# Sums of weights for seven-product tiles, made in DRAM by added transfers

## The chip, the cores and the metric

The kernel runs on one core of one Trainium2 chip. The metric is device microseconds from the start to the end of one execution; the time shown is the median of several runs. A profile is one further execution, taken by the hardware profiler, and its span runs from the first to the last instruction of the core.

Engines are named as in the profile: PE is TensorE, DVE VectorE, ACT ScalarE, POOL GpSimd, SP SyncE. SP and POOL are used here only as queues that issue DMA transfers.

## The reference, cut to what matters

A decoder layer on x of 512 tokens by 1024 channels, all in float32:

```python
f = swiglu(rms_norm(h, ffn1_norm_pre), ffn1_w_gate, ffn1_w_up, ffn1_w_down)
h = h + 0.5 * rms_norm(f, ffn1_norm_post)

u = rms_norm(h, mix_norm_pre)
proj = u @ w_in                     # q, k, v of 12 heads, xr, yr, two gates
...                                 # dilated attention in 3 groups, merged; RG-LRU recurrence
h = h + rms_norm(merged @ w_out, mix_norm_post)

f = swiglu(rms_norm(h, ffn2_norm_pre), ffn2_w_gate, ffn2_w_up, ffn2_w_down)
h = h + 0.5 * rms_norm(f, ffn2_norm_post)

def swiglu(x, w_gate, w_up, w_down):
    return (jax.nn.silu(x @ w_gate) * (x @ w_up)) @ w_down
```

The inner width of each feed-forward is 2816, that is 22 tiles of 128 columns (f = 0 to 21), each with 128 columns of `w_gate` and 128 of `w_up`.

## The kernel before, in words

**Precision by splitting.** Each float32 operand is split into a rounded part and a rest (`split`: ACT copies to a 32-bit format with fewer bits, DVE subtracts), and a product is made of three matmuls: high by high, high by low, low by high. So all weights pass ACT and DVE before PE reads them.

**Seven products in place of eight.** Most tiles with two weight blocks (gate and up of a feed-forward tile; pairs of columns of `w_in`) are computed in Strassen-Winograd fashion. The two blocks and the two halves of the depth give four quarters of weights, u0, u1, g0, g1, each 128 x 512 as stored; two halves of the tokens and the two halves of the depth give four quarters of activations. `seven` makes seven products (p1, p2, p6, p5, p7, p4, p3 in this order, 12 matmuls of 256 columns each) in place of eight. It needs forms of the weights: u0+u1, u0+u1+g0, u0+u1+g0+g1, u0+g0, and g0, g1 (in the kernel before, p4 takes u1 and p3 the sum of all four). `w_forms(key)` makes them: one load of all four quarters (1 MB) into a buffer `raw`, four VectorE adds of 128 x 512 (lines 567, 568, 569 and 572), some of them in place in `raw`, and splits into three buffers `w8` and one `w4`. There are 51 such tiles: 17 in the first feed-forward (f = 5 to 21), 16 pairs in the mixers, 18 in the second feed-forward (f = 4 to 21). `NSTD` gives the number of tiles of each feed-forward that are computed plainly.

**Stages, in order.** First feed-forward (`ffn(1, ...)`), ended by `last_product`: the last down-projection, whose result is multiplied by a row of gains on DVE, added to the residual h, normalised and transposed (`Boundary`: `block`, `turn`). Then attention (`values`, `qk`, `attend` for four heads, `seven` tiles for the gates), the recurrence (`conv`, `branch`, `gates_of`, `recur`), the output projection with the second `Boundary`, and the second feed-forward. In a feed-forward the order is that of `ffn_order`: the forms of tile f+1 are prepared ahead of the products of tile f; after some tiles one half of an earlier part's down-projection is done (`down`).

**Loads of weights.** All weights lie in one DRAM tensor `wst` (`in_w` in the profile) in the order of use; `raw_of` loads them group by group on SP's queue into a ring `raw` of two slots of 128 x 2048. A slot comes free when the last split or add that reads it is done. `w8` has four buffers, `w4` two.

**POOL's queue.** It issues only DMA transfers: at the end of the first feed-forward the residual (`h` from `in_xn`, line 745), two rows of gains (`gains`, line 397), the new residual to DRAM (`kept_m`, line 432), a reordering of the values of one group (line 812); after attention the residual back (line 981), and the same kinds of transfers around the second boundary.

**What sets the order.** The kernel is written for a planner. Instructions get numbers in the order in which the code issues them; a block under `tc.high_priority(offset=n)` gets numbers that are n lower. The planner plays the program through with costs of its own and gives each engine or queue, whenever it is free, the ready instruction with the lowest number. Ready means that what it reads has been written and that a buffer for what it writes is free. From this it fixes one order for each queue and the semaphore waits; on the chip each queue then runs strictly in that order. A DRAM tile of its own name and tag has its own place, and needs no other to be released.

Of the kernel before, what the change touches and what calls it, by code (L numbers as in the profile page):

```python
# [10 lines left out]
F32 = mybir.dt.float32  # L11
F32R = mybir.dt.float32r
AF = mybir.ActivationFunctionType
ALU = mybir.AluOpType
AX = mybir.AxisListType

P = 128
# [3 lines left out]
NF = 22  # L21
FF_PARTS = ((0, 4), (4, 8), (8, 12), (12, 16), (16, 22))
NSTD = {1: 5, 2: 4}
# [4 lines left out]
RAW_W = 2048  # L28
NEG = -1.0e30
AHEAD = 100  # L30
# [100 lines left out]
def stream_groups():  # L131

    groups, cur, w = [], [], 0
    for key, width in stream_plan():
        if w + width > RAW_W or (cur and cur[0][0][0] == "start"):
            groups.append(cur)
            cur, w = [], 0
        cur.append((key, w, width))
        w += width
    groups.append(cur)  # L140
    return groups
# [12 lines left out]
def hybrid_layer(ctx: ExitStack, tc: tile.TileContext, xT: bass.AP, xN: bass.AP, wst: bass.AP,  # L154
                 first: bass.AP, rows: bass.AP, consts: bass.AP, bias: bass.AP, out: bass.AP):
    nc = tc.nc
# [4 lines left out]
    wpool = ctx.enter_context(tc.tile_pool(name="wpool", bufs=4))  # L161
# [3 lines left out]
    dpool = ctx.enter_context(tc.tile_pool(name="dpool", bufs=1, space=bass.MemoryType.DRAM))  # L165
# [35 lines left out]
    groups = stream_groups()  # L201
    state = {"g": 0, "i": 0, "off": 0, "raw": None}

    def raw_of(key):

        g, i = state["g"], state["i"]
        grp = groups[g]
        if i == 0:
            w = grp[-1][1] + grp[-1][2]
            raw = wpool.tile([P, RAW_W], F32, name="raw", tag="raw", bufs=2)  # L210
            src = bass.AP(tensor=wst.tensor, offset=wst.offset + state["off"], ap=[[w, P], [1, w]])
            nc.sync.dma_start(raw[:, :w], src)
            state["raw"] = raw
            state["off"] += w * P
        k, o, w = grp[i]
        assert k == key, (k, key)
        src = state["raw"][:, o:o + w]
        if i + 1 == len(grp):
            state["g"], state["i"] = g + 1, 0
        else:  # L220
            state["i"] = i + 1
        return src

    def fetch(key, slot=None, ahead=0):

        with tc.high_priority(offset=ahead if slot else AHEAD):
            src = raw_of(key)
            w = src.shape[-1]
            t = slot() if slot else w8() if w > 512 else w4()
            split(t[:, 0, :w], t[:, 1, :w], src)  # L230
            return t[:, 0, :w], t[:, 1, :w]

    def w8():
        return wpool.tile([P, 2, 1024], F32R, name="w8", tag="w8", bufs=4)

    def w4():
        return wpool.tile([P, 2, 512], F32R, name="w4", tag="w4", bufs=2)
# [27 lines left out]
    def split(dh, dl, src):  # L265
        ACT.activation(dh, src, AF.Copy)  # L266
        DVE.tensor_sub(dl, src, dh.bitcast(F32))  # L267

    def acc_ps():
        return psum.tile([P, T], F32, name="acc", tag="acc", bufs=5)  # L270

    def aux_ps():
        return psum.tile([P, T], F32, name="aux", tag="aux", bufs=3)

    def tmp(name):
        return tpool.tile([P, T], F32, name=name, tag="t")
# [280 lines left out]
        return t, [early, middle, late]  # L557

    spool = [None]

    def w_forms(key):

        with tc.high_priority(offset=AHEAD):
            raw = raw_of(key)
            u0, u1, g0, g1 = (raw[:, i * 512:(i + 1) * 512] for i in range(4))
            s12 = spool[0].tile([P, 2, 512], F32, name="s12", tag="s", bufs=2)
            DVE.tensor_add(s12[:, 1, :], u0, u1)
            DVE.tensor_add(s12[:, 0, :], s12[:, 1, :], g0)
            DVE.tensor_add(u0, u0, g0)
            a, b, c, d = w8(), w8(), w8(), w4()  # L570
            split(a[:, 0, :], a[:, 1, :], raw[:, 1024:2048])
            DVE.tensor_add(g1, s12[:, 0, :], g1)  # L572
            split(b[:, 0, :], b[:, 1, :], s12.rearrange("p s c -> p (s c)"))
            split(c[:, 0, :], c[:, 1, :], raw[:, 0:1024])
            split(d[:, 0, :], d[:, 1, :], g1)
            lo, hi = slice(0, 512), slice(512, 1024)
            return {"p1": a[:, :, lo], "p2": a[:, :, hi], "p6": b[:, :, lo], "p5": b[:, :, hi],
                    "p7": c[:, :, lo], "p4": c[:, :, hi], "p3": d}
# [114 lines left out]
    def act_two(pool):  # L693

        ts = [pool.tile([P, 8, T], F32R, name="act", tag="act", bufs=3) for _ in range(2)]
        return Act([ts[0][:, k, :] for k in range(8)], [ts[1][:, k, :] for k in range(8)])
# [22 lines left out]
    u1 = act_two(ap1)  # L719
# [9 lines left out]
    for k in range(KC):  # L729
        wh, wl, raw = wts[k]  # L730
# [30 lines left out]
    with ExitStack() as mx:  # L761
# [14 lines left out]
        def values(g, first=False):  # L776
            if g:
                vals[g] = apool.tile([P, 4, T], F32, name="vals", tag=f"v{g}")
            else:
                vals[g] = tpl.tile([P, 8, T], F32, name="vals", tag="attn")[:, 0:4, :]  # L780
            ws = [fetch(("v", g, k)) for k in range(4)] if first else [None] * 4
            pss = [acc_ps() for _ in range(4)] if g != VALUES[1] else [aux_ps(), aux_ps(), aux_ps(), acc_ps()]

            def part(kk, bs):
                wh, wl = (w.rearrange("p (k c) -> p k c", k=2) for w in ws[kk])
                for b in bs:
                    bl = slice(b * P, (b + 1) * P)
                    for i in range(2):
                        k = 2 * kk + i
                        PE.matmul(pss[b], um.hi[k][:, bl], wh[:, i, :], start=k == 0, stop=False)  # L790
                        PE.matmul(pss[b], um.hi[k][:, bl], wl[:, i, :], start=False, stop=False)  # L791
                        PE.matmul(pss[b], um.lo[k][:, bl], wh[:, i, :], start=False, stop=k == KC - 1)  # L792

            if first:
                for b in range(4):
                    for kk in range(4):
                        part(kk, (b,))
                    if b < 2:
                        bd1.turn(b + 2)
                    ACT.activation(vals[g][:, b, :], pss[b], AF.Copy)  # L800
            else:
                for kk in range(4):
                    ws[kk] = fetch(("v", g, kk))
                    part(kk, range(4))
                for b in range(4):
                    ACT.activation(vals[g][:, b, :], pss[b], AF.Copy)
            if g == 0:

                nv = apool.tile([P, 4, T], F32, name="vals", tag="vn")
                for b in range(4):  # L810
                    for p in range(4):
                        nc.gpsimd.dma_start(nv[32 * p:32 * p + 32, b, :], vals[g][32 * b:32 * b + 32, p, :])
                vals[g] = nv

        t, steps = forms_of(um, um_t[:2], um_t[2:], apool, False)
        values(VALUES[0], True)
        attn_t = tpl.tile([P, 8, T], F32R, name="attn", tag="attn")
        attn = Act([attn_t[:, i, :] for i in range(4)], [attn_t[:, 4 + i, :] for i in range(4)])
        steps[0]()
        values(VALUES[1])  # L820
        steps[1]()
        values(VALUES[2])
        pairs = [[(g * 4 + hd, 12 + g * 4 + hd) for g in range(NG)] for hd in range(NH)]
# [140 lines left out]
            DVE.tensor_sub(attn.lo[hd], om, attn.hi[hd].bitcast(F32))  # L964

        for hd in range(NH):
            attend(hd, qkvs.pop(hd))
            if hd + 1 < NH:
                qkvs[hd + 1] = qk(hd + 1)


        for c in range(0, KC, 2):
            g, u = tmp("g"), tmp("u")
            seven(t, pair_of(("pair", 52 + c, 53 + c)), acc_ps()[:, :HB], [g[:, h] for h in HALVES],
                  [u[:, h] for h in HALVES])
            ACT.activation(facc[:, c, :], g, AF.Sigmoid)
            ACT.activation(facc[:, c + 1, :], u, AF.Sigmoid, scale=-1.0)
# [9 lines left out]
    with ExitStack() as mx:  # L987
# [10 lines left out]
        o, w = SMALL["ap"]  # L998
# [42 lines left out]
        def branch(hd):  # L1041

            gel = []
            for c in (2 * hd, 2 * hd + 1):
                ps = acc_ps()
                gemm(ps, fetch(("in", 44 + c)), um)
                ge = lpool.tile([P, T], F32, name="ge", tag="ge", bufs=4)
                with tc.high_priority(offset=EVAC):
                    DVE.tensor_copy(ge, ps)
                gel.append(ge)  # L1050
            return gel
# [47 lines left out]

        conv(0)  # L1100
        for hd in range(NH):
            gel = branch(hd)
            if hd + 1 < NH:
                conv(hd + 1)
            gas, gxs = gates_of(hd)
            recur(hd, gel, gas, gxs)
            for c in GATE1[hd]:
                ps = acc_ps()
                gemm(ps, fetch(("in", 60 + c)), um)
                ACT.activation(sig[:, c, :], ps, AF.Sigmoid)  # L1110
# [28 lines left out]
    grow5, _ = gains(ap2, 4)  # L1139
# [121 lines left out]
```

## Time and profile before

| | |
|---|---|
| median of 3 runs | 1248.76 us (1248.39 to 1249.63) |
| span of the profiled execution | 1246.4 us |
| PE busy | 1233.0 us (99%) |
| DVE busy | 913.5 us (73%) |
| ACT busy | 670.4 us (54%) |
| POOL busy | 26.2 us (2%) |
| DMA, mean over the span | 113 GB/s |
| granted TensorE clock, mean | 0.998 |

The span is what the profiler sees of one execution; the time of a run has some 2 us around it. In the lines of the profile, "L267" is a line of the kernel (often that of a helper, such as `split`), "w<-raw" what it writes and reads by the program's names, and "<-" in square brackets or behind a bar what ended the engine's idle time before it. SPq and POOLq are the queues' instructions that issue transfers, and "us to landing" is from the issue to the last byte.

### The profile page before, as it was taken

The page shows a single profiled execution, that of the slowest core. Times are in us where ns is not written, and L with a number is a line of the kernel's source. Part 1 is how long each engine was busy: PE and PEld are TensorE (multiplying, and loading weights), DVE is VectorE, ACT ScalarE, POOL GpSimd, SP SyncE. Part 2 cuts the span into 40 slices and gives each one's busy share as a digit, 9 for nine tenths or more (in the row PEclk, how much of TensorE's full clock was granted, in tenths as well). Part 3 has the DMA queues.
Part 4 walks back from the last instruction along what each step waited for, and adds up shares of the span by engine and source line. Part 5 has one row for each costly group of instructions (what it writes and reads, how often), then busy time and mean ns, then how long its engine had stood idle before and what let it go on. Part 6 is the DMA issues. An engine that isn't in the chain of part 4 may idle for free.

```text
span 1246.4 us, 18979 instructions
## 1 busy us (share of the span) xinstructions
PE 1233.0 (99%) x7712; PEld 1115.6 (90%) x7712; DVE 913.5 (73%) x1447; ACT 670.4 (54%) x1105; POOL 26.2 (2%) x51
## 2 busy tenths in 40 slices
PE   9999999999999999999999999999999999999997
PEld 8899999999878899999987787888899999999986
DVE  7996777786576588888565877664795867777755
ACT  7555444445355465666536979634564544445432
POOL 0000000000002000000000000000100000000000
PEclk9999999999999999999999999999999999999999
DMA  6222222235414222231342122224451322222241
GB/s 242 103 85 104 102 104 103 102 114 200 167 74 144 102 81 98 77 111 69 121 151 101 68 101 102 101 101 169 141 166 67 136 102 102 102 102 73 101 183 67
DMA packets 27383, 141.37 MB, mean 113 GB/s; under 512 B 2976, under 2 KB 6176, under 8 KB 13216
## 3 DMA queue, kind: packets, MB, share of 16 engines
q1 hardware_dynamic: 20016, 122.86, 27.4%
q0 software_dynamic: 7280, 17.30, 4.1%
q8 instruction: 60, 0.98, 0.3%
q14 instruction: 27, 0.22, 0.1%
HBM read 129.67 MB, written 6.29 MB: 109 GB/s over the span
## 4 chain that ended last, share of the span: by engine, by line
PE 89%; DVE 5%; ACT 4%; issue 1%; DMA 0%; SPq 0%; DVEq 0%; ACTq 0%
PE acc L591 11%; PE acc L592 11%; PE acc L593 11%; PE acc L385 7%; PE acc L387 7%; PE acc L386 7%; PE acc L281 7%; PE acc L280 6%; PE acc L279 6%; PE aux L592 3%; PE aux L591 3%; PE aux L593 3%; PE acc L790 1%; PE acc L792 1%; PE acc L791 1%
## 5 line engine op out<-in xcount | busy, mean ns | idle before, releaser
L267 DVE TENSOR_TENSOR w<-raw,w 128x1024 fp32r<-128x1024 f32 (+1 forms) x240 | 256.7, 1073 | 111.2 <-ACT w L266 79.4
L266 ACT ACTIVATE w<-raw 128x1024 fp32r<-128x1024 f32 (+1 forms) x240 | 224.5, 939 | 176.9 <-DVE raw L572 59.8
L591 PE MATMUL acc<-big,w 128*128 128x256 f32 x880 | 250.8, 285 | 0.0
L592 PE MATMUL acc<-big,w 128*128 128x256 f32 x880 | 249.9, 284 | 0.0
L593 PE MATMUL acc<-big,w 128*128 128x256 f32 x880 | 249.6, 284 | 0.0
L591 PEld LDWEIGHTS acc<-big,w 128*128 128x128 f32 x880 | 168.6, 192 | 0.9
L592 PEld LDWEIGHTS acc<-big,w 128*128 128x128 f32 x880 | 168.7, 192 | 0.6
L593 PEld LDWEIGHTS acc<-big,w 128*128 128x128 f32 x880 | 168.7, 192 | 0.0
L598 ACT ACTIVATE c<-acc 128x256 f32<-128x256 f32 x169 | 64.1, 379 | 80.0 <-PE acc L593 76.4
L386 PE MATMUL acc<-wd,act 128*128 128x512 f32 x256 | 99.8, 390 | 0.0
L385 PE MATMUL acc<-wd,act 128*128 128x512 f32 x256 | 99.6, 390 | 0.0
L387 PE MATMUL acc<-wd,act 128*128 128x512 f32 x256 | 99.4, 389 | 0.0
L591 PE MATMUL aux<-big,w 128*128 128x256 f32 x280 | 79.2, 283 | 0.0
L592 PE MATMUL aux<-big,w 128*128 128x256 f32 x280 | 79.2, 283 | 0.0
L593 PE MATMUL aux<-big,w 128*128 128x256 f32 x280 | 79.2, 283 | 0.0
L591 PE MATMUL acc<-tx,w 128*128 128x256 f32 x268 | 76.1, 284 | 0.0
L592 PE MATMUL acc<-tx,w 128*128 128x256 f32 x268 | 75.8, 283 | 0.0
L593 PE MATMUL acc<-tx,w 128*128 128x256 f32 x268 | 75.8, 283 | 0.0
L281 PE MATMUL acc<-big,w 128*128 128x512 f32 x192 | 74.7, 389 | 0.0
L280 PE MATMUL acc<-big,w 128*128 128x512 f32 x192 | 74.7, 389 | 0.0
L279 PE MATMUL acc<-big,w 128*128 128x512 f32 x192 | 74.7, 389 | 0.0
L267 DVE TENSOR_TENSOR w<-s,w 128x1024 fp32r<-128x1024 f32 x51 | 62.4, 1224 | 10.1 <-ACT w L266 10.1
(314 smaller groups left out, 2762.1 us busy)
## 6 DMA issues: line engine op xcount, KB each, us to landing
raw<-in_w SPq DMA_DIRECT2D x110, 1024.0 KB, 4.8
big<-act POOLq DMA_DIRECT2D x6, 512.0 KB, 3.3
gains<-in_rows POOLq DMA_DIRECT2D x5, 512.0 KB, 5.0
h<-in_x SPq DMA_DIRECT2D x8, 256.0 KB, 5.2
h<-in_xn POOLq DMA_DIRECT2D x4, 512.0 KB, 7.0
kept_m<-h POOLq DMA_DIRECT2D x4, 512.0 KB, 2.9
h<-kept_m POOLq DMA_DIRECT2D x4, 512.0 KB, 5.6
kept<-h POOLq DMA_DIRECT2D x4, 512.0 KB, 3.3
```

What stands on the lines that cost most here:

```text
L266: ACT.activation(dh, src, AF.Copy)
L267: DVE.tensor_sub(dl, src, dh.bitcast(F32))
L279: PE.matmul(ps, wh, xh, start=first, stop=False)
L280: PE.matmul(ps, wh, xl, start=False, stop=False)
L281: PE.matmul(ps, wl, xh, start=False, stop=last)
L385: PE.matmul(ps, x.hi[k][:, bl], wh, start=k == 0, stop=False)
L386: PE.matmul(ps, x.hi[k][:, bl], wl, start=False, stop=False)
L387: PE.matmul(ps, x.lo[k][:, bl], wh, start=False, stop=k == x.n - 1)
L591: PE.matmul(ps, wh, xh, start=start and k == 0, stop=False, skip_group_check=True)
L592: PE.matmul(ps, wh, xl, start=False, stop=False, skip_group_check=True)
L593: PE.matmul(ps, wl, xh, start=False, stop=k == 3, skip_group_check=True)
L598: ACT.activation(c, ps, AF.Copy)
```

## The change

Only the 18 seven-product tiles of the second feed-forward are touched. For each of them `sums_ahead` makes four sums of quarters in a DRAM tile of its own, by four transfers on POOL's queue: one copy of u0 into all four places, and three transfers that add to what is there (u1 to three places, g0 to three, g1 to one), each of which waits for the one before. The calls stand in the attention (ten tiles) and in the recurrence (eight). When the second feed-forward comes to such a tile, `w_forms_made` takes the place of the old `w_forms`: it loads three quarters (u1, g0, g1) and the four sums, each into a slot of the ring `raw`, and splits them; the four VectorE adds are gone. The third `w8` buffer now holds the forms of p3 and p7, and the `w4` buffer that of p4.

```diff
-    def raw_of(key):
+    def raw_of(key, skip=0):
...
-            src = bass.AP(tensor=wst.tensor, offset=wst.offset + state["off"], ap=[[w, P], [1, w]])
-            nc.sync.dma_start(raw[:, :w], src)
+            src = bass.AP(tensor=wst.tensor, offset=wst.offset + state["off"] + skip, ap=[[w, P], [1, w - skip]])
+            nc.sync.dma_start(raw[:, :w - skip], src)
...
+    made = {}
+
+    def place_of(key):
...
+    def sums_ahead(f):
+
+        key = ("gu", 2, f)
+        off, w = place_of(key)
+
+        def stored(i, n):
+            return bass.AP(tensor=wst.tensor, offset=wst.offset + off + i * 512, ap=[[w, P], [0, n], [1, 512]])
+
+        t = dpool.tile([P, 4, 512], F32, name=f"sums{f}", tag=f"sums{f}")
+        nc.gpsimd.dma_start(t, stored(0, 4))
+        nc.gpsimd.dma_start(t[:, 0:3, :], stored(1, 3), accum_op=ALU.add)
+        nc.gpsimd.dma_start(t[:, 1:4, :], stored(2, 3), accum_op=ALU.add)
+        nc.gpsimd.dma_start(t[:, 2:3, :], stored(3, 1), accum_op=ALU.add)
+        made[key] = t
+
+    ahead = list(range(NSTD[2], NF))
+
+    def some_ahead(n=1):
+        for _ in range(n):
+            if ahead:
+                sums_ahead(ahead.pop(0))
+
+    def w_forms_made(key):
+
+        with tc.high_priority(offset=AHEAD):
+            raw = raw_of(key, 512)
+            u1, g0, g1 = (raw[:, i * 512:(i + 1) * 512] for i in range(3))
+            sums = wpool.tile([P, RAW_W], F32, name="sums", tag="raw", bufs=2)
+            nc.sync.dma_start(sums, made[key].rearrange("p s c -> p (s c)"))
+            a, b, c, d = w8(), w8(), w8(), w4()
+            split(a[:, 0, :], a[:, 1, :], raw[:, 512:1536])
+            split(d[:, 0, :], d[:, 1, :], u1)
+            split(b[:, 0, :], b[:, 1, :], sums[:, 0:1024])
+            split(c[:, 0, :], c[:, 1, :], sums[:, 1024:2048])
+            lo, hi = slice(0, 512), slice(512, 1024)
+            return {"p1": a[:, :, lo], "p2": a[:, :, hi], "p5": b[:, :, lo], "p6": b[:, :, hi],
+                    "p3": c[:, :, lo], "p7": c[:, :, hi], "p4": d}
...
     def w_forms(key):
 
+        if key in made:
+            return w_forms_made(key)
...
         values(VALUES[0], True)
+        some_ahead()
...
         values(VALUES[1])
+        some_ahead()
...
         for hd in range(NH):
+            some_ahead()
             attend(hd, qkvs.pop(hd))
...
         for c in range(0, KC, 2):
+            some_ahead()
...
         for hd in range(NH):
+            some_ahead(2)
             gel = branch(hd)
```

More of the change, by code (lines that the diff above doesn't have):

```diff
@@ L559, in hybrid_layer @@
     spool = [None]
+    made = {}
+    def place_of(key):
+        off = 0
+        for grp in groups[1:]:
+            if grp[0][0][0] == "start":
+                off += 512 * P
+                continue
+            w = grp[-1][1] + grp[-1][2]
+            for k, o, _ in grp:
+                if k == key:
+                    return off + o, w
+            off += w * P
+        raise KeyError(key)
+    def sums_ahead(f):
[28 more added lines that the diff above has]
+                    "p3": c[:, :, lo], "p7": c[:, :, hi], "p4": d}
     def w_forms(key):
+        if key in made:
+            return w_forms_made(key)
         with tc.high_priority(offset=AHEAD):
```

## The prediction

> **What bounds the kernel now.** I read the page first: who is busy, and of what the chain of waits is made.
>
> ```profile
> span 1246.4 us, 18979 instructions
> PE 1233.0 (99%) x7712; PEld 1115.6 (90%) x7712; DVE 913.5 (73%) x1447; ACT 670.4 (54%) x1105; POOL 26.2 (2%) x51
> PE 89%; DVE 5%; ACT 4%; issue 1%; DMA 0%; SPq 0%; DVEq 0%; ACTq 0%
> ```
>
> TensorE is the bound: 1233.0 of 1246.4 us busy, and no transfer on the chain. The span is 2.4 us below the median of the runs, 1248.76; I add 2.4 to every span that I work out. An average hides where a change can act, so next comes the view of busy time by stretches: the start, the first feed-forward (FF1), its end, the mixers, the second feed-forward's tiles (FF2), the tail.
>
> ```profile
> 2.50:15.50 13.00, 12.92 (x59) 10.86 (x59) 10.01 (x20) 11.94 (x28) 0.00 (x0) 1.00 1.03 384
> 16.00:300.00 284.00, 284.00 (x1888) 262.84 (x1888) 228.58 (x328) 144.82 (x220) 0.00 (x0) 1.00 0.29 104
> 300.00:345.00 45.00, 45.00 (x236) 38.82 (x235) 26.57 (x38) 18.77 (x30) 3.29 (x6) 1.00 0.59 220
> 345.00:870.00 525.00, 520.85 (x3069) 461.02 (x3068) 375.67 (x634) 313.80 (x528) 13.30 (x26) 1.00 0.30 104
> 925.00:1225.00 300.00, 300.00 (x2034) 279.20 (x2033) 212.84 (x305) 138.24 (x218) 2.69 (x5) 1.00 0.29 104
> ```
>
> The columns are length, then busy time of PE, weight load, DVE, ACT and POOL, granted clock, DMA share and GB/s. In 925 to 1225, where the edited tiles run, PE has no idle time, at full clock, while DVE idles 87 of 300 us. So relief of DVE there buys nothing. What can move the time is a wait that the new transfers make elsewhere.
>
> **The change part by part.** *Removed:* 18 tiles (f = 4 to 21) lose four VectorE adds each.
>
> ```profile
> L568 DVE TENSOR_TENSOR s<-s,raw 128x512 f32<-128x512 f32 x51 | 34.9, 683 | 0.4
> L572 DVE TENSOR_TENSOR raw<-s,raw 128x512 f32<-128x512 f32 x51 | 34.7, 681 | 0.0
> ```
>
> 18 x 4 x 0.683 = 49 us of DVE, covered by PE's 300.00 of 300.00: worth 0.
>
> *Loads in FF2:* each tile's 1024 KB load becomes one of 768 KB and one of 1024 KB (the sums), both from the ring "raw" of two slots. The sums wait for their last add, which is done hundreds of us earlier. The ring is the question.
>
> ```profile
> 956.00 0.33 SPq L212 DMA_DIRECT2D raw<-in_w  x1
> 966.19 0.33 SPq L212 DMA_DIRECT2D raw<-in_w  x1
> 971.00 1.04 ACT L266 ACTIVATE w<-s 128x1024 fp32r<-128x1024 f32 x1
> raw<-in_w SPq DMA_DIRECT2D x110, 1024.0 KB, 4.8
> raw<-in_w SPq DMA_DIRECT2D x1, 1024.0 KB, 8.2
> ```
>
> SyncE issues the next load as a slot comes free, one per tile, 10.19 us apart. With the change the slot free at 966.19 takes the next tile's sums: landed 4.8 us later, at 971.0, just when ACT splits them today (971.00). They feed the third of seven products of the tile after, most of a pitch later. So 0 at a landing of 4.8. At 8.2 (the one load that ran beside POOL's four h loads) ACT's queue would stand 3.4 us with PSUM copies behind it; PE might lose 2 us in each of some 10 tiles that no down-projection follows. Bounds 0 and +20; I take 0, since nothing else transfers there. A gain is excluded by PE's missing idle time.
>
> *Added:* 72 POOL transfers, DRAM to DRAM, for each tile 1024, 768, 768 and 256 KB in rows of 2 KB. **Where they run is my main choice.** They are written into attention and recurrence, but they read only the weights and write tiles of their own. The planner gives a queue whatever is ready, lowest number first, and these are ready at time zero. The profile has a precedent on SyncE:
>
> ```profile
> 372.99 0.33 SPq L859 DMA_DIRECT2D bs<-in_bias  x1
> 380.67 2.60 SPq L212 DMA_DIRECT2D raw<-in_w  x2
> 300.86 1.19 POOL L745 DMA_DIRECT2D h<-in_xn  x2 [300.41 <-PE acc L593]
> 302.52 1.05 POOL L745 DMA_DIRECT2D h<-in_xn  x2 [0.47 <-issue]
> 319.02 1.05 POOL L397 DMA_DIRECT2D gains<-in_rows  x2 [15.45 <-PE acc L387]
> 345.89 0.54 POOL L432 DMA_DIRECT2D kept_m<-h  x1 [25.82 <-DVE h L431]
> 454.08 0.43 PE aux L867 x2
> ```
>
> The first attention bias, wanted by scores at 454, went out at 372.99 ahead of value weights that the code asks for earlier. And POOL has no work before 300.86. So I expect all 72 at the head of POOL's queue, from time 0, beside FF1, and what waits behind them is the residual h, the gains, and the kept_m stores.
>
> *How long the 72 take.* Nothing in the trace transfers DRAM to DRAM or adds. Nearest rows:
>
> ```profile
> 891.38 0.76 POOL L533 DMA_DIRECT2D big<-act  x1 [2.80 <-DVE tx L267]
> 892.13 0.55 POOL L432 DMA_DIRECT2D kept<-h  x1
> 895.50 0.74 POOL L533 DMA_DIRECT2D big<-act  x1 [2.82 <-issue]
> big<-act POOLq DMA_DIRECT2D x6, 512.0 KB, 3.3
> kept_m<-h POOLq DMA_DIRECT2D x4, 512.0 KB, 2.9
> ```
>
> The copy at 895.50 stood 2.82 us with no visible reason; it is the second of 512 rows (128 x 4 pieces) in a short time, and it started 4.12 us after the first, whose kind lands in 3.3. I read: a POOL transfer of that many rows starts only when the one before has landed, plus 0.8. The new copy has 512 rows too, the adds 384, 384 and 128. At the start's 384 GB/s, 1024 KB move in 2.7 us, which leaves 2.1 of the 4.8 as fixed. A transfer then costs 2.1 + moving + 0.8: the copy 5.6; an add of 768 KB 4.9 if it moves its bytes once, 6.9 if it must also fetch the sum so far; the last 3.6 or 4.2. A tile: 19.0 or 23.6. SyncE holds the engines 0.29 of the time in FF1, so the moving part (7.4 or 12.1) grows by 2.1 or 3.5. Eighteen tiles: 381 or 488 us. If two were in flight always, half of the fixed 2.9 would go: 18 x (21.1 - 4 x 1.45) = 275. I take 395: serial, near the cheap add, with some adds overlapping.
>
> On the add's price a page differs from my choice: the Trainium skill, Collectives: The Full Stack, "The bandwidth ceiling", says that a reduce reads two sources and runs at half a copy's rate. By it alone the sum is the 488, and the time 1417.
>
> *What is late then.*
>
> ```profile
> 324.20 0.69 DVE L413 TENSOR_TENSOR facc<-acc,facc 128x512 f32<-128x512 f32 x1 [0.63 <-PE acc L387]
> 325.74 0.69 DVE L417 TENSOR_TENSOR facc<-facc,gains 128x512 f32<-128x512 f32 x1 [0.85 <-ACT sq L378]
> 328.89 1.22 DVE L267 TENSOR_TENSOR w<-raw,w 128x1024 fp32r<-128x1024 f32 x1
> 340.52 0.69 DVE L413 TENSOR_TENSOR facc<-acc,facc 128x512 f32<-128x512 f32 x1 [0.79 <-PE acc L387]
> 344.31 1.28 DVE L431 SCALAR_TENSOR_TENSOR h<-facc,stat,h 128x1024 f32<-128x1024 f32 x1
> L397 POOL DMA_DIRECT2D gains<-in_rows x5: 527/530/531, 319.0 to 1204.8; - x5
> gains<-in_rows POOLq DMA_DIRECT2D x5, 512.0 KB, 5.0
> ```
>
> DVE multiplies by the gains at 325.74, in order; behind it stand the evacuations of FF1's last product and the value weights' splits. PE goes on into its five "acc" banks, to about 340.5, then stops. Freed at T, POOL issues four h loads and two gains (six at 0.55: 3.3 us); the gains land 5.0 later; DVE then has its backlog of 325.74 to 340.52: three L413 and four L417 at 0.69 and four splits at 1.22, 9.7 us. So PE starts again at T + 18.0, and the loss is T + 18.0 - 340.5, about T - 322: 73 us at T = 395, 0 below 322. The h needed at 344.31 has landed by then. kept_m and the rest of POOL's queue move along.
>
> *The start.* The transfers meet the one stretch where SyncE fills the engines (share 1.03 in 2.5 to 15.5).
>
> ```profile
> 2.11 4.73 DMA h<-in_x
> 8.43 0.50 PE acc L280
> 8.93 0.23 PE acc L281
> ```
>
> PE waits for the second h slice, which takes 4.73 us; with half the bandwidth its moving part doubles: +2. After that a slice costs PE 12 x 0.23 = 2.8 us and brings 512 KB, 2.7 us at half of 384 GB/s: just covered. +2, bounds 0 and +8. FF1's weight loads may land in 8.2 in place of 4.8; the cover is DVE's 55 idle us in 16 to 300. I take 0, bound +5.
>
> **Sum:** 1246.4 + 73 + 2 = 1321.4 of span, 1324 us.
>
> **The rivals.** (1) *The chain is done in time.* Transfers overlap: at T = 275 nothing waits, and only the start's +2 stays: 1251 us, no measurable loss or just one. It decides at T = 322: 17.9 us for a tile, 4.5 for a transfer. Against it is the 2.82 us stand; for it, that adds have fewer rows. The Trainium skill, DMA: Bandwidth & Descriptors, "Anatomy of one DMA", gives 2.0 us plus bytes at 436 GB/s: an estimate by it of 4.4, 3.8, 3.8 and 2.6 us, 263 us for all, so this rival. (2) *They stay where they are written.* POOL is then free from 346 to past 870 but for 13.30 busy us; 18 x 21.1 = 380 fits in 525, and later uses are far away: 1249 us, no change. Against it is the bias row. (3) *Adds much dearer:* T above 488, time above 1417. (4) *The ring:* in time at the boundary, but FF2 loses up to 20 in ACT's queue: to 1271. (5) *Faster,* since DVE is 49 us lighter: PE's idle time in FF2 is 0.00, so under 1 us.
>
> **How the numbers follow.** Forecast (T from 325 to 488, time 1253 to 1417) 0.50; (1) 0.24; (2) 0.08; (3) 0.10; (4) 0.05; (5) 0.03. Within 0.2% (2.5 us, about what a measurement can tell) are (2) and 0.14 of (1): 0.22. Slower: 0.50 + 0.10 + 0.05 + 0.10 = 0.75. The range of 1249 to 1417 leaves out (3) and most of (2) and (5), under 2 in 10; the likeliest case's own range is 1253 to 1417.
>
> **What would show it.** POOL's first transfer before 2 us; h<-in_xn issued near 395 and not at 300.86, and as late as the last sum; PE idle some 70 us between 325 and 420; the adds at L567 to L572 down from 51 to 33; PE still 100% in FF2. h<-in_xn at 301 would make me wrong on the loss; sums issued after 350 would make me wrong on where they run.

## The result and the profile after

The changed kernel takes 1502.13 us (median of 4 runs, 1497.72 to 1505.31), the kernel before 1248.6: 1.202 times as long, 95% interval 1.200 to 1.2045. The profiled run of the changed kernel has a span of 1503.3 us, 256.9 more than before. The prediction said 1324, between 1249 and 1417: the right sign and, as will be seen, the right place, but far too little.

The page of the changed kernel: span, busy engines, the chain of waits, the queues (packets, MB, share of the 16 DMA engines over the span) and, at the end, the transfers' median time from issue to landing.

```profile
span 1503.3 us, 19100 instructions
PE 1246.7 (83%) x7712; PEld 1122.9 (75%) x7712; DVE 874.9 (58%) x1375; ACT 670.3 (45%) x1105; POOL 99.9 (7%) x123
PEclk9999999999555555999999999999999999999999
PE 54%; issue 34%; POOL 5%; DVE 4%; ACT 2%; DMA 1%; DVEq 0%; POOLq 0%; ACTq 0%
q0 software_dynamic: 29168, 69.21, 24.9%
sums<-in_w POOLq DMA_DIRECT2D x36, 768.0 KB, 9.7
sums<-in_w POOLq DMA_DIRECT2D x18, 1024.0 KB, 10.4
```

PE is busy 13.7 us longer with the same 7712 matmuls (1246.7 against 1233.0); the other 243 us of the longer span are idle time of PE. The chain was 89% PE and now has 34% "issue" (an instruction stood and the profile shows no reason) and 5% POOL. DVE lost 38.6 us of its 913.5.

The order of time on POOL, with the idle time before each row and its releaser in brackets:

```profile
1.31 0.85 POOL L585 DMA_DIRECT2D sums<-in_w  x1 [0.87 <-POOLq L1311]
...
476.58 1.24 POOL L586 DMA_DIRECT2D sums<-in_w  x1 [7.81 <-issue]
485.34 1.22 POOL L586 DMA_DIRECT2D sums<-in_w  x1 [7.52 <-issue]
...
569.65 1.69 POOL L588 DMA_DIRECT2D sums<-in_w  x2 [8.81 <-issue]
570.76 2.23 POOL L800 DMA_DIRECT2D h<-in_xn  x3
...
578.30 0.53 POOL L397 DMA_DIRECT2D gains<-in_rows  x1 [2.35 <-issue]
```

All 72 transfers stand at the head of POOL's queue, from 1.31 on, one after the other (only some of the 256 KB adds overlap a copy). The loads of h, before issued at 300.86, follow at 570.76, right behind the last of them, and the gains behind those. What waits for the gains is seen on DVE, in the order of time:

```profile
348.29 0.69 DVE L413 TENSOR_TENSOR facc<-acc,facc 128x512 f32<-128x512 f32 x1 [0.63 <-PE acc L387]
584.62 0.69 DVE L417 TENSOR_TENSOR facc<-facc,gains 128x512 f32<-128x512 f32 x1 [235.64 <-DMA gains<-in_rows]
```

and on PE, in the view of waits (waiter, what it waited for, us in total, times, longest):

```profile
PE acc L385 <- DVE facc L413: 217.3, 1, 217.3
```

The view by stretches, with the columns that the prediction explains, for FF1, the stall and most of FF2:

```profile
16.00:300.00 284.00, 274.18 (x1736) 249.32 (x1735) 220.58 (x319) 139.54 (x216) 34.16 (x33) 0.98 0.83 193
345.00:590.00 245.00, 27.69 (x115) 22.42 (x114) 7.37 (x9) 5.39 (x11) 35.16 (x37) 0.56 0.65 113
1200.00:1450.00 250.00, 249.81 (x1805) 236.89 (x1804) 151.18 (x206) 124.45 (x196) 2.16 (x4) 1.00 0.45 158
```

DVE's first multiplication by the gains comes at 584.62 instead of 325.74, so 258.9 us late; the whole kernel is 256.9 us late. Nothing is lost behind this place, and in FF2 (last row) PE is as full as before. The 258.9 are made of 24.1 us lost before the place is reached (L413 at 348.29 instead of 324.20; PE is no longer full in 16 to 300) and of 235.64 us of waiting for the gains. At these two times PE has done the same 2095 matmuls, so the 24.1 can be split (a row of the kernel before, then one of the changed kernel):

```profile
0.00:324.20 324.20, 323.07 (x2095) 297.17 (x2096) 253.04 (x368) 168.40 (x263) 3.50 (x10) 1.00 0.34 125
0.00:348.29 348.29, 330.84 (x2095) 301.05 (x2096) 254.71 (x367) 168.54 (x263) 42.75 (x46) 0.98 0.83 193
```

PE's idle time grew by 16.3 us, and the same matmuls took 7.8 us longer, at a mean granted clock of 0.98 instead of 1.00.

### The profile page after: what moved, and what is told of

It reads as the page before. It is cut to its first block, busy times and chain, and to the rows that moved or that the text cites. A ratio compares the mean times of both kernels' runs of the same rounds, so it can differ in the third digit from the quotient of the medians.

```text
span 1503.3 us, 19100 instructions
## 1 busy us (share of the span) xinstructions
PE 1246.7 (83%) x7712; PEld 1122.9 (75%) x7712; DVE 874.9 (58%) x1375; ACT 670.3 (45%) x1105; POOL 99.9 (7%) x123
## 4 chain that ended last, share of the span: by engine, by line
PE 54%; issue 34%; POOL 5%; DVE 4%; ACT 2%; DMA 1%; DVEq 0%; POOLq 0%; ACTq 0%
PE acc L646 6%; PE acc L647 6%; PE acc L648 6%; PE acc L281 5%; PE acc L279 5%; PE acc L280 5%; PE acc L386 3%; PE acc L387 3%; PE acc L385 3%; POOL sums L586 1%; POOL sums L587 1%; POOL sums L585 1%; PE aux L646 1%; PE aux L647 1%; PE aux L648 1%
## 5 line engine op out<-in xcount | busy, mean ns | idle before, releaser
L267 DVE TENSOR_TENSOR w<-raw,w 128x1024 fp32r<-128x1024 f32 (+1 forms) x222 | 234.4, 1063 | 109.6 <-ACT w L266 90.7
L266 ACT ACTIVATE w<-raw 128x1024 fp32r<-128x1024 f32 (+1 forms) x222 | 204.4, 929 | 180.8 <-DMA raw<-in_w 43.1
L385 PE MATMUL acc<-act 128*128 128x512 f32 x16 | 8.3, 516 | 217.3 <-DVE facc L413 217.3
L385 PEld LDWEIGHTS acc<-act 128*128 128x128 f32 x16 | 4.1, 256 | 218.6 <-DVE facc L413 217.7
L417 DVE TENSOR_TENSOR facc<-facc,gains 128x512 f32<-128x512 f32 x12 | 8.3, 689 | 240.5 <-DMA gains<-in_rows 235.6
L378 ACT ACTIVATE sq<-facc 128x512 f32<-128x512 f32 x16 | 10.1, 631 | 269.6 <-DVE facc L413 264.6
```

Source lines behind the costliest of these rows:

```text
L385: PE.matmul(ps, x.hi[k][:, bl], wh, start=k == 0, stop=False)
```

## The experiments

My theory: POOL's queue is in order, so the loads that the boundary needs stand behind 18 tiles x 31.6 us (570 us, from the rows above). The rivals: the DMA engines are too full for anything else (contention), or FF2 itself became slower. And what made 31.6 us of a tile that I had put at 21 or so?

**Boundary transfers off POOL.**

```diff
-            nc.gpsimd.dma_start(t[:, j, :], bass.AP(tensor=rows.tensor, offset=rows.offset + i * D,
+            nc.sync.dma_start(t[:, j, :], bass.AP(tensor=rows.tensor, offset=rows.offset + i * D,
...
-            nc.gpsimd.dma_start(self.kept[b], hb(b))
+            nc.sync.dma_start(self.kept[b], hb(b))
...
-        nc.gpsimd.dma_start(hb(b), xN[b])
+        nc.sync.dma_start(hb(b), xN[b])
```

The vals copies and the loads of h from kept_m and kept are changed in the same way; the sums stay on POOL.

> The sums and their 72 transfers stay at the head of POOL's queue from time 0; the loads of h and of the gains, the stores of kept_m and kept, and the small vals copies are issued on SP instead. Theory (the loads of h and gains stand behind the sums in POOL's queue): the stall of 217 us before the first post-norm is gone, the sums still end near 570, and what stays is what the transfers cost by sharing the DMA engines at the start and in the first feed-forward (the changed kernel reached that place 24 us later than the kernel before): 1249 + 24 = 1273, between 1255 and 1290. Rival (the DMA engines are so full that FF1's and the boundary's loads are late from whichever queue): over 1400. Rival (the second feed-forward itself is slower with sums read from DRAM): over 1300 with the loss after 925.

Measured: 1302.94 us, ratio 1.0433 (1.0388 to 1.0478). In its trace the last sums are issued at 605, later than in the changed kernel, and DVE does not wait for the gains (order of time, POOL and DVE):

```profile
605.11 1.70 POOL L588 DMA_DIRECT2D sums<-in_w  x2 [9.54 <-issue]
367.00 0.69 DVE L417 TENSOR_TENSOR facc<-facc,gains 128x512 f32<-128x512 f32 x1 [0.85 <-ACT sq L378]
```

and by stretches:

```profile
420.00:650.00 230.00, 216.09 (x1570) 206.25 (x1569) 165.67 (x299) 116.66 (x249) 24.01 (x24) 0.97 0.72 166
```

So four fifths of the loss are the queue's order. The expectation was 30 us short on the rest. The profiled execution, the longest of the four runs, is 62.1 us longer than before: the boundary is 41.3 us late without any wait for the gains, and 13.7 us more of PE are missing between 420 and 650 (229.75 before). How much of this is the loads that I put into SP's queue was not separated.

**Fewer tiles ahead.** `ahead = list(range(NF - 12, NF))`, and `NF - 9`; the other tiles keep the old `w_forms`.

> Only the last 12 of the 18 tiles get their sums ahead; the first 6 are added on VectorE as in the kernel before. Theory (head of POOL's queue, 31.6 us a tile): the sums end at 12 x 31.6 = 380, the gains land 14 us later at 394, the place that needs them is reached near 349, so the stall falls from 236 to 45 us; with the 24 us lost before it and up to 12 us after it 1249 + 45 + 24..36 = 1318 to 1330. Rival (loss in proportion to the transfers' bytes): 1249 + 253 x 12/18 = 1418. Rival (cost in the second feed-forward by the ring of raw slots, 12 of 18 tiles): the same 1418, lost after 925.

> Only the last 9 of the 18 tiles get their sums ahead. Theory: the sums end at 9 x 31.6 = 285, before the 349 at which the first post-norm needs its gains, so no stall is left there; only the start and the first feed-forward pay for the shared DMA engines: 1249 + 15..24 = 1264 to 1273. Rival (loss in proportion to the transfers' bytes): 1249 + 253 x 9/18 = 1375.

Measured: 1335.72 us (ratio 1.0693, 1.0673 to 1.0712) with 12 tiles and 1281.5 (1.0265, 1.0248 to 1.0282) with 9; in proportion to the bytes it would be 1418 and 1375. The order of time on POOL and DVE, with 12 tiles and then with 9:

```profile
397.21 2.22 POOL L800 DMA_DIRECT2D h<-in_xn  x3
411.51 0.69 DVE L417 TENSOR_TENSOR facc<-facc,gains 128x512 f32<-128x512 f32 x1 [55.25 <-DMA gains<-in_rows]
```

```profile
301.17 0.85 POOL L588 DMA_DIRECT2D sums<-in_w  x1 [9.60 <-DMA sums<-in_w]
332.27 1.16 POOL L800 DMA_DIRECT2D h<-in_xn  x2 [30.25 <-PE acc L648]
357.11 0.69 DVE L417 TENSOR_TENSOR facc<-facc,gains 128x512 f32<-128x512 f32 x1 [0.85 <-ACT sq L378]
```

With 9 tiles the sums are out at 301, POOL idles 30 us until PE frees the slots of h, and nobody waits for the gains; still L417 is 31.4 us later than before, and the span 32.0. That rest is not the queue's order. It lies before the boundary, in the start and FF1. The expectations had 24 us for it, so both were missed by under ten.

**More descriptor space.** In the changed kernel a transfer starts as the one before lands, even where it works on another tile.

```diff
-    nc = _bacc.Bacc("TRN2", target_bir_lowering=False, num_devices=1, dynamic_dma_scratch_size=1024)
+    nc = _bacc.Bacc("TRN2", target_bir_lowering=False, num_devices=1, dynamic_dma_scratch_size=2048)
...
-CB = 6
+CB = 5
```

> The space for the descriptors that GpSimd writes is doubled (1024 to 2048 bytes a partition); one of six small work tiles goes to make room. It tells why a transfer's pitch equals its landing time. Theory (the descriptor space holds one large transfer, so each waits for the one before): two are in flight, the sums end earlier, at best by the engines' share of 0.65 at 0.65 x 571 = 371, stall 36 instead of 236 us: 1300 to 1420. Rival (each transfer waits for its predecessor's data or semaphore): the pitch and the time stay, 1495 to 1510. Rival (two in flight share the same rate, the DRAM side being the limit): pitch unchanged in pairs, also near 1500, but with landings of 16 to 18 us instead of 9 to 10.

Measured: 1341.25 us, ratio 1.0739 (1.0713 to 1.0766). The order of time on POOL and DVE, and then a stretch of FF1:

```profile
380.98 0.80 POOL L588 DMA_DIRECT2D sums<-in_w  x1 [8.40 <-DMA sums<-in_w]
388.10 1.13 POOL L800 DMA_DIRECT2D h<-in_xn  x2 [6.32 <-PE acc L648]
414.28 0.69 DVE L417 TENSOR_TENSOR facc<-facc,gains 128x512 f32<-128x512 f32 x1 [0.85 <-ACT sq L378]
```

```profile
200.00:350.00 150.00, 130.31 (x887) 122.80 (x888) 98.10 (x142) 61.22 (x97) 31.56 (x31) 0.94 0.99 228
```

The stand without a reason was descriptor space: with twice of it the waits are for the sums' own data, and the last sums are issued at 381 in place of 570. The time lies in the theory's range, but not for its reason, a stall of 36 us at best: nobody waits for the gains any more; L417 is 88.5 us late since FF1 itself is slow, with the DMA engines busy 0.99 of the time. The control for the missing work tile:

> The kernel before with five of the small work tiles "c" in place of six: the control for the run with doubled descriptor space, which gave one of them up. Theory (the 88 us which that run lost in the first feed-forward came from its DMA engines, busy 0.99 of the time): 1247 to 1251. Rival (the missing work tile held up PSUM's evacuation and is part of the 88 us): over 1255.

Measured: 1247.44 us, ratio 0.9987 (0.9978 to 0.9996). With nothing else changed the missing work tile costs nothing; its effect beside the added transfers was not tested apart.

So there are two costs. The loads of FF1's weights show the second. Their landing in 50 to 300, before, after, with 9 tiles and with twice the descriptor space (a row of the view of transfers in each of the four kernels):

```profile
raw<-in_w SPq DMA_DIRECT2D x25, 1024.0 KB, 4.8
```

```profile
raw<-in_w SPq DMA_DIRECT2D x24, 1024.0 KB, 7.4
```

```profile
raw<-in_w SPq DMA_DIRECT2D x24, 1024.0 KB, 7.5
```

```profile
raw<-in_w SPq DMA_DIRECT2D x20, 1024.0 KB, 11.0
```

The Trainium skill, DMA: Bandwidth & Descriptors, "Issuing engines are not separate DMA queues", says that transfers run on the same 16 DMA engines whichever engine issued them; the traces agree: 4.8, 7.4 and 11.0 us for one and the same load. ACT, which splits the weights, feels it: its waits for these loads in 16 to 300, before and after (total, times, longest):

```profile
ACT w L266 <- DMA raw<-in_w: 3.6, 1, 3.6
ACT w L266 <- DMA raw<-in_w: 24.8, 10, 6.6
```

**Held back to where the calls stand.**

```diff
-                        nc.gpsimd.dma_start(nv[32 * p:32 * p + 32, b, :], vals[g][32 * b:32 * b + 32, p, :])
+                        behind[0] = nc.gpsimd.dma_start(nv[32 * p:32 * p + 32, b, :], vals[g][32 * b:32 * b + 32, p, :])
...
-            nc.gpsimd.dma_start(hb(b), kept_m[b])
+            behind[0] = nc.gpsimd.dma_start(hb(b), kept_m[b])
...
-                sums_ahead(ahead.pop(0))
+                with tc.issue_after(behind[0].ins):
+                    sums_ahead(ahead.pop(0))
```

> Order alone is changed: the sums of the ten attention steps are held behind the last vals copy in POOL's queue (385 in the kernel before), those of the eight recurrence steps behind the loads of h from kept_m, so the transfers run where the change's words put them. Theory (POOL's queue is in order, 31.6 us a tile): the first boundary is as before (no stall at the first post-norm, reached at 324); the sums end at 385 + 18 x 31.6 = 954 at the earliest; the gains and kept stores of the second boundary, needed at 852, stand behind them, so the stall moves there: 954 + 13 - 852 = 115 us; with 10 to 25 us for the shared DMA engines in attention and recurrence 1249 + 125..140 = 1374 to 1389. Rival (the loss of after was the first feed-forward's DMA traffic and not the order): 1260 to 1290, with no stall at the second boundary. Rival (the planner puts them at the head all the same): near 1502.

> As the held-back kernel, and the gains and the kept stores of both boundaries are issued on SP, so that nothing of the second boundary stands behind the sums. Theory: neither boundary stalls; left are the shared DMA engines between 385 and 954: 1249 + 10..35 = 1260 to 1285, and the second feed-forward at its former length, since PE sets its pace with or without VectorE's adds. Rival (VectorE's 49 us of adds were worth something in the second feed-forward): below 1249. Rival (the sums come too late for the second feed-forward): over 1300 with PE idle after 925.

Measured: 1375.66 us (ratio 1.1011, 1.0996 to 1.1026) as held back, and 1315.82 (1.0517, 1.0494 to 1.0539) with gains and kept stores moved. Held back alone, in the order of time:

```profile
325.75 0.69 DVE L417 TENSOR_TENSOR facc<-facc,gains 128x512 f32<-128x512 f32 x1 [0.85 <-ACT sq L378]
975.73 1.66 POOL L397 DMA_DIRECT2D gains<-in_rows  x2
985.29 0.69 DVE L417 TENSOR_TENSOR facc<-acc,gains 128x512 f32<-128x512 f32 x1 [111.69 <-DMA gains<-in_rows]
```

The first boundary is back at its old time, and the stall of 112 us (115 expected) is at the second one. The rival of 1260 to 1290 without a stall falls. The second kernel was to take at most 1285. Its view of waits names what I had left on POOL:

```profile
PE acc L648 <- DMA big<-act: 27.4, 2, 26.5
PE acc L649 <- DMA big<-act: 5.8, 2, 2.9
```

The SBUF copies of L533, due when FF2 begins, stand behind the sums too: 33 of the 69 us, the same mechanism a third time. Of the rest PE misses 7.8 us in 420 to 650, where raw loads land in 8.2 us instead of 4.7, and 9.6 in 650 to 930. Most of the other 18.5 us is PE's own time: the same 7712 matmuls took 1249.1 us instead of 1233.0, at a mean granted clock of 0.973 instead of 0.998.

```profile
PE 1249.1 (95%) x7712; PEld 1128.0 (86%) x7712; DVE 874.2 (66%) x1375; ACT 670.3 (51%) x1105; POOL 93.0 (7%) x110
```

These 16.1 us leave 2.4 that I did not assign.

**Held back, and so few that nothing is late.**

> The last 12 tiles only, held back behind the vals copies as before; nothing else is moved. Theory (two costs: what stands behind the sums in POOL's queue, and the 16 DMA engines shared with the weight loads): the sums run from 385 to about 385 + 12 x 33 = 781, before the second boundary's gains at 847, so no load or store stands behind them when it is due; what is left is the sharing of the DMA engines during attention and recurrence, where the held-back kernel lost 10.2 us of PE between 420 and 650 and 5.7 between 650 and 870, and a few us of slower clock after each stall: 1249 + 12..25 = 1261 to 1274. Rival (order is the whole loss): 1247 to 1252. Rival (relief of VectorE in the second feed-forward is worth 12/18 of its 49 us once nothing is late): 1216 to 1235.

> As before with the last 6 tiles only. Theory: the sums run from 385 to 385 + 6 x 33 = 583 and share the DMA engines with the loads of attention alone: 1249 + 6..13 = 1255 to 1262. Rival (order is the whole loss): 1247 to 1252. Rival (VectorE's relief counts): 1232 or less.

Measured: 1261.08 us (ratio 1.0102, 1.0077 to 1.0127) with 12 tiles, 1255.86 (1.0056, 1.0044 to 1.0068) with 6. In both the sums end (at 792 and 584) before anything behind them is waited for. The remaining loss grows with the bytes moved beside the loads, and VectorE's lighter load brings nothing visible; both rivals fall.

**The second feed-forward's part alone.**

> Only the second feed-forward's part of the change: it reads 768 KB of a tile's block and a second load of 1024 KB, and VectorE adds nothing; the transfers that make the sums are left out, and the second load reads the stored block in their place. Theory (PE sets the pace there, the adds lay beside it): 1249, within 2 us, VectorE busy 40 to 50 us less. Rival (the ring of two raw slots holds the loads up): 1252 to 1270, PE idle after 925. Rival (relief of VectorE is worth something): 1200 to 1246.

Measured: 1248.78 us, ratio 0.9998 (0.9990 to 1.0007); DVE is busy 874.4 us instead of 913.5. Neither the ring of two slots nor the relief shows.

**What makes a transfer take 9 us.**

> The changed kernel with the same 72 transfers of the same number of rows, each row 128 bytes in place of 2 KB, so a sixteenth of the bytes; the sums are left out (the second feed-forward loads the stored block in their place). What sets a transfer's 5.9 to 8.9 us, its bytes, its rows or a fixed part? If bytes alone (with the 2.1 us that the 64 KB vals copies show): 72 x 2.2 = 160, over before h is due at 301, and the DMA engines are nearly free: 1248 to 1256. If a fixed part and bytes (a line through 5.9 at 256 KB and 8.7 at 1024 KB has 5.0 at none): 72 x 5.05 = 364, the gains at 378 instead of 585, so 1502 - 207 = 1295, between 1280 and 1325. If rows (the same descriptors take the same time): near 1502.

Measured: 1250.77 us, ratio 1.0013 (1.0004 to 1.0022). Minimum, median and maximum landing, first of the changed kernel between 400 and 560, where nothing else moves (lines 585, 586, 587, 588 in this order), then of the short rows over the whole run:

```profile
DMA to landing us min/median/max: 8.3/8.7/11.3
DMA to landing us min/median/max: 8.0/8.9/9.6
DMA to landing us min/median/max: 8.1/9.0/9.8
DMA to landing us min/median/max: 5.2/5.9/7.4
```

```profile
DMA to landing us min/median/max: 2.7/2.8/5.7
DMA to landing us min/median/max: 3.2/3.4/8.1
DMA to landing us min/median/max: 3.3/3.4/8.0
DMA to landing us min/median/max: 2.3/2.6/7.5
```

It is the bytes. With the same number of rows the copy lands in 2.8 instead of 8.7, the adds in 3.4 instead of 8.9; the short ones ran beside FF1's loads, so alone they would be no slower. The 960 KB between the two copies take 5.9 us, 167 GB/s; the 720 KB between the adds take 5.5 us, 134 GB/s. Half of the six copies overlapped a 256 KB add; the three issued alone landed in 8.3 to 8.6, so 167 is if anything low. An add moves its bytes at about 0.8 of a copy's rate. The loads from DRAM into SBUF had moved at 384. The 72 short transfers are over before 250 (not 160, since most take 2.6 to 3.4 us instead of 2.2), and the kernel is 2 us longer than before. ACT's waits for raw loads in 16 to 300 are back at 3.7 us. So the second cost, too, goes with the bytes and not with the number of transfers.

> A list of prices, in the changed kernel's order; the sums' values are left out (the first copy takes the block as it is stored, in rows of 8 KB, and the second transfer copies where it added). Landing times are read by line in the stretch from 400 on, where the changed kernel showed 8.7 us for the 1024 KB copy in 2 KB rows, 8.9 for a 768 KB add and 5.9 for a 256 KB add. Theory A (an add is dear for its second read): the plain 768 KB copy lands in about 2.1 + 0.75 x 6.6 = 7.0, the 8 KB rows change nothing (8.7), adds stay 8.9. Theory B (2 KB rows are dear): the 8 KB-row copy lands in 4 to 6 (a load of 1024 KB into SBUF shows 4.1 to 4.8), the plain 768 KB copy stays at 7 to 8.9. Theory C (DRAM to DRAM is slow whatever the rows and the operation): 8.7, and 7.0 to 8.9 for both kinds.

Measured: 1357.6 us, one run. In 355 to 424 the lines are the 1024 KB copy in 8 KB rows, the plain 768 KB copy, and the 768 KB add:

```profile
DMA to landing us min/median/max: 9.5/11.6/13.8
DMA to landing us min/median/max: 8.2/9.8/11.4
DMA to landing us min/median/max: 9.0/9.5/12.2
```

The plain copies and the adds landed in about the same time (9.8 and 9.5), but this does not price a plain copy alone: the two copies were issued 5.4 us apart, at 388.95 and 394.34, and overlapped, while the adds went one at a time. Alone it was not measured; my estimate from the 2.8 us and 167 GB/s above is 7.1 us for 768 KB. The long rows are no quicker. Two of them were in flight at a time: two copies of 1024 KB and two adds of 256 KB, issued from 378.5 to 380.1, had landed by 394.3, which is 2.62 MB in 15.8 us, 166 GB/s, with the reserve that FF1's loads still shared the first part of this stretch. That speaks against theory B. A and C are both true in part: transfers within DRAM are slow as such, and an add is dearer than a copy by about a quarter. Why DRAM to DRAM has this rate stays open.

## Why the prediction was wrong

**Where and how: right.** All 72 transfers at the head of POOL's queue from before 2 us; h, gains and the stores behind them; PE idle in one piece of 217 us; FF2 unchanged, the relief and the ring worth 0 (the part alone is 0.9998). The sum itself holds: 1246.4 + (T - 322) + 2 with the measured T of 571 gives 1497.4 of span; measured 1503.3.

**The step that failed is the price of a transfer, so T: 395 taken, 571 measured.** A tile was put at 19.0 to 23.6 us without SyncE's share, 21.1 to 27.1 with it; it cost 28.2 in 400 to 570, where nothing else moved, and 31.6 on average. Within it the fixed 2.1 us was about right (2.8 for 64 KB), the 0.8 between transfers did not exist, and the moving rate was wrong: I carried 384 GB/s, which loads into SBUF showed, over to transfers within DRAM, which move at 134 to 167. I had written that no row of the trace showed such a transfer, and then bounded it by the two readings of one number. The upper bound of 488 was no bound; rival (3) held it to be 0.10 likely and named the adds alone. The adds are the dearer kind (134 against 167 GB/s), but the copy, which has no second source, was as far off: 5.6 us taken with the 0.8, 8.7 measured. The Trainium skill, Collectives: The Full Stack, "The bandwidth ceiling", by which 488 came out, has a reduce at half a copy's rate. In number 488 came nearer, but the ratio here is 0.8. The Trainium skill, DMA: Bandwidth & Descriptors, "Anatomy of one DMA", gives an estimate of 4.4 us for the 1024 KB copy. The 8.7 us measured show that it does not hold for this kind of transfer.

**The overlap that I counted on as a possible gain** would not have saved the time: with two in flight T is 381, near my 395, and the kernel takes 1341, not 1324 or less, since then FF1 pays.

**A second term was too small and did no harm:** the start and FF1, +2 with bounds of +8 and +5. The place was reached 24 us late, and 31 and 88 us late in the kernels above. The start took some 7 us of the 24 (51 matmuls done at 20 us instead of 84, then the same pace up to 40), within its bound; FF1 took the other 17, far beyond its +5. In the changed kernel this is hidden in the wait for the gains, which ends at a time that T alone sets; where T is short it is the whole loss. What fell is the cover, "DVE's 55 idle us in 16 to 300": loads landing in 7.4 us, not even the 8.2 reckoned with, leave PE busy for 274.18 of 284 us.

## What to carry to other kernels

Ask of every transfer that waits for nothing where a planner will put it and what comes later in the same in-order queue: here the work was free on its engine, and three different stages in turn waited behind it. Price a kind of transfer only from a row of that kind; DRAM to DRAM is not DRAM to SBUF, and without a row the range must reach much further up than the two nearest guesses. And before moving work off an engine, look whether that engine sets the pace in the stage: 39 us less of VectorE were worth nothing in a stage in which TensorE never idles.

## What was new of the hardware

- Transfers within DRAM landed in 8.7 us for 1024 KB with nothing else moving, 167 GB/s by the differences above; adding in the transfer moved 134, so it cost about a quarter more per byte.
- GpSimd's transfers of 384 or 512 rows went one at a time with 1024 bytes of descriptor space and overlapped with 2048: the 72 were issued within 381 us instead of 570, and the DMA engines' share rose from 0.83 (16 to 300) to 0.99 or more.
- The granted clock of TensorE was lower in stretches in which it idled in part or in the main: 0.56 in the stall (345 to 590), 0.83 in the first 20 us, 0.98 in 16 to 300. The same matmuls then took longer, 13.7 us in all in the changed kernel and 16.1 in the held-back kernel with gains and stores moved. What the stall's low clock cost behind it does not show in the changed kernel: it is 258.9 us late at the end of the stall and 256.9 at its end.
